# Later residual stores, and another split of the up and gate products in a two-layer decoder trunk

## The chip, the core and the metric

The kernel runs on one core of one Trainium2 chip. The metric is the device time of one execution in microseconds (us). Before the change three executions took 2463.84 us in the median (2461.32 to 2466.27). A further execution was recorded by the hardware profiler; the times in the views below are of that one. The engines are named as the profile names them: PE (matrix products), PEld (its weight loads), DVE (elementwise work and 32x32 transposes), ACT (activations and copies), POOL (here the issuing of small transfers) and SP (the issuing of large ones).

## The reference

Two layers, each with two residual additions, over 256 positions of width 2048 in float32. The mixer half of a layer projects the normed input with `w_in`, runs windowed attention and a spatial gating unit, merges the two by gates, and adds `merged @ w_out` to x. The half that the change touches is this:

```
h2 = rms_norm(x, ffn_norm[l])
x = x + (jax.nn.silu(h2 @ w_gate[l]) * (h2 @ w_up[l])) @ w_down[l]
```

`w_gate` and `w_up` are 2048 x 5632, `w_down` is 5632 x 2048.

## The kernel before, in words

Precision. Each float32 operand is split into a high part and the rest (`whi`/`wlo` for weights, `uh`/`ul` for activations), and each product is three matmuls: high by high, rest by high, high by rest (lines 399, 400, 401). ACT makes `whi` by a copy (line 256), DVE makes `wlo` by a subtraction (line 264). The weights come from memory once and are split once, so for each 256 x 512 piece of weight there is one ACT operation, one DVE operation and a run of matmuls.

Jobs, units, parts. The work is a list of jobs. A wide job multiplies all 256 positions by 1024 columns of a weight, in units of 512 rows (four units for a weight with 2048 rows). A unit is done in one of two ways. Plain: four quarters, each of 12 matmuls of 128x512. Or by a seven-product scheme in the manner of Strassen: seven products of 6 matmuls each, 42 in place of 48. For that the weight's blocks must be added first: four DVE operations of 128x1024 (line 240), and there are seven splits in place of four. The activations need sums too (`sh`, `sl`, lines 520 to 508), made once for a unit and used by all jobs that take that unit in seven products. A job's `m` says how many of its units are done so; they come first, in an order given by `HEAD` and `TAIL`, with the four sums of a unit placed by `SUM_AT` some parts ahead of their use. A job with m=0 has 192 matmuls, with m=1 186, with m=2 180. I call the products and the quarters parts; a part's `whi` and `wlo` are made ahead of PE, as far as 6 and 5 buffers go.

The half that is touched. The columns of gate and up are taken in rounds of 4, 4 and 3 blocks of 512 (`ROUNDS`), with blocks counted f = 0 to 10. In a round come pairs: gate for blocks f and f+1, then up for the same blocks; the last block (f = 10) has gate and up in one job. After the pairs of a round two down jobs add into x. The gate's results leave PSUM through ACT (line 1088), the up's through DVE (line 1094); the result `hid` is transposed in 32x32 blocks by DVE (line 483, tile `blk`), and 16 small transfers issued by POOL (line 489, tile `tt`) put the blocks in their places. ACT and DVE split what arrived (lines 587 and 590, or 511 to 523 with the sums).

The residual before it. The two jobs of `merged @ w_out` add into the four 512-column pieces of x on DVE (line 997). Each piece is then transposed and gathered in the same manner (`blk`, `tt`), scaled on ACT (line 583) and split into one unit of h2 (`uh`, `ul`); all four units are needed by the first gate job. The first two also get their sums. Each piece is stored in memory by SP (`keep_x`, line 359, tile `kept`) and fetched again for the next residual (line 356).

Order. The order of each engine's instructions is fixed by the program. A clock of slots ticks one for each quarter and a half for each product; `after(n, fn)` puts an operation n slots later in every engine's order. How late the second piece of a job is evicted and transposed depends on the m of the next job (`behind`, with `T1_LATE` and `UNIT_LATE`). SP's queue holds the weight loads (line 220), which wait for one of 5 buffers, and between them the stores and fetches of x, in one order.

Of the kernel before, what the change touches and what calls it, by code (L numbers as in the profile page):

```python
# [31 lines left out]
CW2 = 2 * CW  # L32
# [5 lines left out]
N_BIG = 25  # L38
G_BUSY, G_LAND = 3.5, 3
T1_LATE, THEN_LATE, UNIT_LATE = (1.5, 3), (3, 7), (3, 3)  # L40
Q_FIRST = 15
Q_STEP = 4
LOAD_BY = (1, 2, 3, 4)
ROUNDS = ((0, 1, 2, 3), (4, 5, 6, 7), (8, 9, 10))
M_OUT, M_FFN, M_DOWN = (0, 1), (2, 1, 1), 1
M_Q = 0
M_GATE, M_ATT, M_SGU = (1, 1, 1, 1), (0, 0), (1, 0)
M_V, M_U = 1, 1
# [4 lines left out]
def hybrid_trunk(ctx: ExitStack, tc: tile.TileContext, x, mix_norm, w_in, q_norm, k_norm, sinks,  # L53
# [37 lines left out]
    NF = FF // CW  # L91
# [16 lines left out]
    sums, uses = {}, []  # L108
# [51 lines left out]
    for l in range(DEPTH):  # L160
        wl = w_in[l]
        for o in (0, None)[::-1 if l == 0 else 1]:
            add_job([wl[:, o:o + CW2]], m=M_Q * l) if o is not None else add_job([wl[:, O_KV:O_KV + CW]])
        for o, m in ((O_V, M_V), (O_U, M_U), (O_GATE, M_GATE[0]), (O_GATE + CW2, M_GATE[1])):
            add_job([wl[:, o:o + CW2]], m=m)
        add_job([wl[:, O_GATE + D:O_GATE + D + CW2]], m=M_GATE[2])
        for i, o in enumerate((0, CW2)):
            add_job([w_attn_branch[l, :, o:o + CW2]], m=M_ATT[i])
        add_job([wl[:, O_GATE + D + CW2:O_GATE + 2 * D]], m=M_GATE[3])
        for i, o in enumerate((0, CW2)):  # L170
            add_job([w_sgu_branch[l, :, o:o + CW2]], m=M_SGU[i])
        for i, o in enumerate((0, CW2)):
            add_job([w_out[l, :, o:o + CW2]], m=M_OUT[i])
        for fs in ROUNDS:
            for f in fs[::2]:
                if f + 1 < NF:
                    for w, m in zip((w_gate, w_up), M_FFN if f else (1, 1)):
                        add_job([w[l, :, f * CW:(f + 2) * CW]], m=m)
                else:
                    add_job([w[l, :, f * CW:(f + 1) * CW] for w in (w_gate, w_up)], m=M_FFN[2])  # L180
            for o in (0, CW2):
                add_job([w_down[l, :, o:o + CW2]], units=list(fs), m=M_DOWN)

    needed = {}
    for i, n in uses:
# [109 lines left out]
    def after(n, fn):  # L295
        steps.append((slot_no[0] + n, fn))
# [53 lines left out]
    def rows(v):  # L350

        return v.rearrange("(t p) n -> p t n", p=P)
# [5 lines left out]
    def keep_x(c):  # L358
        nc.sync.dma_start(rows(kept[c]), xt[c])
        home[c] = kept[c]  # L360
# [403 lines left out]
    class Attention:  # L764
# [62 lines left out]
        def begin(self):  # L827
            n = Q_FIRST
            for c in range(2):
# [139 lines left out]
    def residual(units, nxt, sums, out_at=None, scale=None):  # L969

        for j in range(0, NCH, 2):

            def done(c, ps, j=j):
                o = j + c

                square_at = 5 if c == 0 else behind(2, 2, 5)

                def then():
                    nxt.unit(o, sums=o < sums)
                    after(square_at, lambda: nxt.squares(o))  # L980
                    if o == NCH - 1:
                        after(square_at + 1, lambda: nxt.finish())

                evicting(c, lambda t: added(o, t, ps), then if nxt is not None else None, late_then=UNIT_LATE)
                if out_at is None:
                    after(7 if c == 0 else 8, lambda: keep_x(o))

            def added(o, t, ps):
                n = 2 if out_at is not None and o == NCH - 1 else 1
                w = CW // n  # L990
                for i in range(n):
                    sl = slice(i * w, (i + 1) * w)
                    d, src = xt[o][:, t, sl], ps[t][:, sl]
                    if scale is None:
                        nc.vector.tensor_tensor(out=d, in0=src, in1=d, op=ALU.add)  # L995
                    else:
                        nc.vector.scalar_tensor_tensor(out=d, in0=src, scalar=scale, in1=d, op0=ALU.mult, op1=ALU.add)  # L997
                    if out_at is not None:
                        eng = nc.sync if i == 0 else nc.scalar
                        eng.dma_start(out_at[0, t * P:(t + 1) * P, o * CW + i * w:o * CW + (i + 1) * w], d)  # L1000

            job = jobs[job_no[0]]
            length = 3.5 * job.m + 4 * (len(job.units) - job.m)
            after(length - 8, lambda j=j: fetch_x(j))
            after(length - 6, lambda j=j: fetch_x(j + 1))
            run(units, done)

    prepare(0)

    for l in range(DEPTH):  # L1010
# [69 lines left out]
        nxt = Norm(mix_cols(l + 1)) if l + 1 < DEPTH else None  # L1080
        for i, fs in enumerate(ROUNDS):
            hid, hT = {}, {}
# [7 lines left out]
            def up_done(f, c, ps):  # L1090
                a = hid[f]

                def upped(t):
                    nc.vector.scalar_tensor_tensor(out=a[:, t, :], in0=ps[t], scalar=norm.r[t], in1=a[:, t, :],
                                                   op0=ALU.mult, op1=ALU.mult)

                evicting(c, upped, lambda: transposed(hT, f, a, on_pe=f == NF - 1, sums=f in fs[:M_DOWN]))

            for f in fs[::2]:
                if f + 1 < NF:  # L1100
# [48 lines left out]
```

## Time and profile before

| what | value |
|---|---|
| median of three executions | 2463.84 us (2461.32 to 2466.27) |
| the profiled execution | 2466.55 us, span 2464.6 us, granted PE clock 0.997 |
| PE busy | 2443.4 us, 10950 matmuls |
| DVE busy | 1990.1 us (81%) |
| ACT busy | 1429.3 us (58%) |
| POOL busy | 475.0 us (19%) |
| read from and written to memory | 492.04 MB, 16.78 MB |

A busy PE is not PE at its peak: matmuls overlap, and a record of 0.39 us can follow the one before it after 0.23 us. So the distance between starts says more than busy time. A window's row gives for each engine the busy time and the count of instructions in it, then the granted PE clock (1.00 is full), the share of the transfer engines that were at work, and GB/s. In a row of the timeline the bracket at the end is the idle time of the engine before it and who ended it.

### The profile page before, as it was taken

To read this page: it belongs to the slowest core of one execution; us is meant where nothing else is said; L and a number is where in the kernel's file an instruction comes from. 1 tells how busy PE (TensorE), PEld (TensorE's weight loads), DVE (VectorE), ACT (ScalarE), POOL (GpSimd) and SP (SyncE) were. 2 spreads that over 40 slices of the span, in tenths; PEclk is the share of its full clock that TensorE was granted. 3 is DMA by queue.
4 is the path that set the end of the run, shared out by engine and by line. 5 is a ranking of instruction groups with operands and counts; after the bars stand their busy time and mean duration, and the time that the engine had idled before them with its cause. 6 is when DMAs were issued, how large, how long until landed. Compare 5 with 4: busy or idle time off the path is not lost. (4 is left out here: it accounts for less than half of the span.)

```text
span 2464.6 us, 30889 instructions
## 1 busy us (share of the span) xinstructions
PE 2443.4 (99%) x10950; PEld 2012.3 (82%) x10950; DVE 1990.1 (81%) x2189; ACT 1429.3 (58%) x1758; POOL 475.0 (19%) x903
## 2 busy tenths in 40 slices
PE   9999999999999999999999999999999999999999
PEld 7888888877888888888888888887778888888887
DVE  7898768786978797788879976777869787978786
ACT  6575545475655665465666665554756555655653
POOL 1421300441220022002235022014402200220020
PEclk9999999999999999999999999999999999999999
DMA  8555556776576757666776546566856757575764
GB/s 311 195 202 190 165 188 218 225 251 216 213 242 205 256 197 243 226 248 198 267 262 218 184 165 201 190 202 205 284 197 222 239 194 263 209 238 190 260 205 166
DMA packets 179051, 539.20 MB, mean 219 GB/s; under 512 B 23872, under 2 KB 26544, under 8 KB 178896
## 3 DMA queue, kind: packets, MB, share of 16 engines
q1 hardware_dynamic: 150832, 508.51, 60.5%
q0 software_dynamic: 27744, 28.44, 3.8%
q8 instruction: 86, 1.41, 0.2%
q14 instruction: 69, 0.57, 0.1%
q10 hardware_dynamic: 320, 0.27, 0.0%
HBM read 492.04 MB, written 16.78 MB: 206 GB/s over the span
## 5 line engine op out<-in xcount | busy, mean ns | idle before, releaser
L264 DVE TENSOR_TENSOR wlo<-raw,whi 128x1024 fp32r<-128x1024 f32 (+1 forms) x956 | 1150.5, 1219 | 381.6 <-PE acc L400 278.6
L256 ACT ACTIVATE whi<-raw 128x1024 fp32r<-128x1024 f32 (+1 forms) x956 | 997.2, 1057 | 692.8 <-PE acc L401 611.9
L399 PE MATMUL acc<-whi,uh 128*128 128x512 f32 x3004 | 1178.0, 392 | 6.8 <-ACT uh L587 4.2
L400 PE MATMUL acc<-wlo,uh 128*128 128x512 f32 x3004 | 1171.1, 390 | 2.4 <-DVE wlo L264 2.4
L401 PE MATMUL acc<-whi,ul 128*128 128x512 f32 x3004 | 1171.7, 390 | 1.4 <-DVE ul L590 1.2
L489 POOL DMA_DIRECT2D tt<-blk x800 | 392.1, 497 | 1682.6 <-DVE blk L483 665.4
L399 PEld LDWEIGHTS acc<-whi,uh 128*128 128x128 f32 x3004 | 565.1, 188 | 128.9 <-ACT uh L587 5.5
L401 PEld LDWEIGHTS acc<-whi,ul 128*128 128x128 f32 x3004 | 565.0, 188 | 121.4 <-DVE ul L590 3.3
L400 PEld LDWEIGHTS acc<-wlo,uh 128*128 128x128 f32 x3004 | 565.2, 188 | 119.8 <-DVE wlo L264 4.0
L399 PE MATMUL acc<-whi,sh 128*128 128x512 f32 x464 | 182.4, 393 | 2.8 <-ACT acc L435 2.2
L256 ACT ACTIVATE whi<-sum 128x1024 fp32r<-128x1024 f32 x116 | 122.8, 1058 | 102.1 <-PE acc L401 87.0
L400 PE MATMUL acc<-wlo,sh 128*128 128x512 f32 x464 | 181.6, 391 | 0.0
L401 PE MATMUL acc<-whi,sl 128*128 128x512 f32 x464 | 181.4, 391 | 0.0
L264 DVE TENSOR_TENSOR wlo<-sum,whi 128x1024 fp32r<-128x1024 f32 x116 | 141.3, 1218 | 6.1 <-PE acc L400 6.1
L399 PEld LDWEIGHTS acc<-whi,sh 128*128 128x128 f32 x464 | 87.5, 188 | 25.7 <-ACT acc L435 6.6
L435 ACT ACTIVATE acc<-acc 128x512 f32<-128x512 f32 x150 | 88.4, 589 | 28.7 <-PE acc L401 20.2
L401 PEld LDWEIGHTS acc<-whi,sl 128*128 128x128 f32 x464 | 87.5, 189 | 18.4
L400 PEld LDWEIGHTS acc<-wlo,sh 128*128 128x128 f32 x464 | 87.5, 189 | 18.0 <-DVE wlo L264 0.3
L590 DVE TENSOR_TENSOR ul<-tt,uh 128x1024 fp32r<-128x1024 f32 x36 | 44.0, 1223 | 42.8 <-ACT uh L587 37.6
L240 DVE TENSOR_TENSOR raw<-raw,sum 128x1024 f32<-128x1024 f32 x58 | 71.0, 1225 | 2.0
L240 DVE TENSOR_TENSOR sum<-raw,raw 128x1024 f32<-128x1024 f32 x58 | 71.0, 1224 | 1.4
L240 DVE TENSOR_TENSOR sum<-raw 128x1024 f32<-128x1024 f32 x58 | 70.7, 1219 | 0.0
(126 smaller groups left out, 1044.5 us busy)
## 6 DMA issues: line engine op xcount, KB each, us to landing
raw<-in_w_in_dram SPq DMA_DIRECT2D x112, 1024.0 KB, 5.5
raw<-in_w_down_dram SPq DMA_DIRECT2D x88, 1024.0 KB, 6.3
raw<-in_w_gate_dram SPq DMA_DIRECT2D x80, 1024.0 KB, 6.3
raw<-in_w_up_dram SPq DMA_DIRECT2D x80, 1024.0 KB, 6.4
raw<-in_w_out_dram SPq DMA_DIRECT2D x32, 1024.0 KB, 6.9
tt<-blk POOLq DMA_DIRECT2D x800, 32.0 KB, 4.9
raw<-in_w_attn_branch_dram SPq DMA_DIRECT2D x16, 1024.0 KB, 6.0
raw<-in_w_sgu_branch_dram SPq DMA_DIRECT2D x16, 1024.0 KB, 5.7
```

Of the source, the lines that this page charges most:

```text
L240: nc.vector.tensor_tensor(out=self.raw(dst), in0=self.raw(one), in1=self.raw(two), op=ALU.subtract)
L256: nc.scalar.activation(hi[:, k, :], raw[:, k, :], AF.Copy)
L264: nc.vector.tensor_tensor(out=lo[:, k, :], in0=raw[:, k, :], in1=hi[:, k, :].bitcast(F32), op=ALU.subtract)
L399: nc.tensor.matmul(ps, a, hi, start=first, stop=False, skip_group_check=True)
L400: nc.tensor.matmul(ps, a, lo, start=False, stop=False, skip_group_check=True)
L401: nc.tensor.matmul(ps, b, hi, start=False, stop=last, skip_group_check=True)
L435: nc.scalar.activation({"11": x, "t2": e, "t3": y}[name], a, AF.Copy)
L489: nc.gpsimd.dma_start(blocks(d)[:, :, i] if whole else d[:, i].rearrange("p k t c -> p (k t) c"), src)
L590: nc.vector.tensor_tensor(out=blocks(unit.lo), in0=tv, in1=blocks(unit.hi).bitcast(F32), op=ALU.subtract)
```

## The change

Three things in the table and two in the code. `keep_x` is put 20 slots after a piece of x is done in place of 7 or 8, in the residuals that feed a norm (the one in the middle of each layer, and the one at the end of the first layer); the others keep 7 and 8. The first gate job of each layer (f = 0) has m=0 in place of 1. The up jobs of f = 0, 2 and 6 have m=2 in place of 1; those of f = 4 and 8 keep 1, and all later gate jobs keep 2. The down jobs' m is now given one by one, with the same values as before.

```diff
+KEEP_LATE = 20
-M_OUT, M_FFN, M_DOWN = (0, 1), (2, 1, 1), 1
+M_OUT, M_FFN, M_DOWN = (0, 1), (2, 2, 1), ((1, 1), (1, 1), (1, 1))
+UP_TWO = (0, 2, 6)
-        for fs in ROUNDS:
+        for fs, ms in zip(ROUNDS, M_DOWN):
             for f in fs[::2]:
                 if f + 1 < NF:
-                    for w, m in zip((w_gate, w_up), M_FFN if f else (1, 1)):
+                    for w, m in ((w_gate, M_FFN[0] if f else 0), (w_up, M_FFN[1] if f in UP_TWO else 1)):
                         add_job([w[l, :, f * CW:(f + 2) * CW]], m=m)
...
-            for o in (0, CW2):
-                add_job([w_down[l, :, o:o + CW2]], units=list(fs), m=M_DOWN)
+            for o, m in zip((0, CW2), ms):
+                add_job([w_down[l, :, o:o + CW2]], units=list(fs), m=m)
...
                 if out_at is None:
-                    after(7 if c == 0 else 8, lambda: keep_x(o))
+                    after(KEEP_LATE if nxt is not None else 7 if c == 0 else 8, lambda: keep_x(o))
...
-                evicting(c, upped, lambda: transposed(hT, f, a, on_pe=f == NF - 1, sums=f in fs[:M_DOWN]))
+                evicting(c, upped, lambda: transposed(hT, f, a, on_pe=f == NF - 1, sums=f in fs[:max(M_DOWN[i])]))
```

The changed file has two more lines near its top, so its line numbers are higher by two: line 264 is 266, 240 is 242, 997 is 999 and so on.

The order moves on DVE where the first gate job begins. `x_4471` (after the change `x_4470`) is the third piece of x, `blk` its transpose, `wlo` the rests of weight parts, `sum` and `raw` as results are the sums of weight blocks, `sums` and `sl` belong to the activations' sums. Before:

```order
L240 TENSOR_TENSOR raw_4380<-raw_4412,sum_4521 128x2x512
L520 TENSOR_TENSOR sums_4375<-tt_4355 128x256
L520 TENSOR_TENSOR sums_4375<-sums_4375,tt_4355 128x256
L520 TENSOR_TENSOR sums_4375<-tt_4355 128x256
L520 TENSOR_TENSOR sums_4375<-tt_4355,sums_4375 128x256
L264 TENSOR_TENSOR wlo_4582<-sum_4521,whi_4559 128x1024
L240 TENSOR_TENSOR sum_4521<-raw_4412,raw_4380 128x1024
L264 TENSOR_TENSOR wlo_4600<-raw_4380,whi_4580 128x1024
L997 SCALAR_TENSOR_TENSOR x_4471<-acc_4273,x_4471 128x512
L997 SCALAR_TENSOR_TENSOR x_4471<-acc_4275,x_4471 128x512
L508 TENSOR_TENSOR sl_4354<-sums_4375,sh_4353 128x1024
L483 STREAM_TRANSPOSE blk_4620<-x_4471 128x4x4x32 x2
```

Now:

```order
L522 TENSOR_TENSOR sums_4375<-tt_4355 128x256
L522 TENSOR_TENSOR sums_4375<-sums_4375,tt_4355 128x256
L522 TENSOR_TENSOR sums_4375<-tt_4355 128x256
L522 TENSOR_TENSOR sums_4375<-tt_4355,sums_4375 128x256
L266 TENSOR_TENSOR wlo_4576<-raw_4380,whi_4554 128x1024
L266 TENSOR_TENSOR wlo_4595<-raw_4412,whi_4574 128x1024
L999 SCALAR_TENSOR_TENSOR x_4470<-acc_4273,x_4470 128x512
L999 SCALAR_TENSOR_TENSOR x_4470<-acc_4275,x_4470 128x512
L510 TENSOR_TENSOR sl_4354<-sums_4375,sh_4353 128x1024
L485 STREAM_TRANSPOSE blk_4615<-x_4470 128x4x4x32 x2
```

The four weight sums of the first gate job are gone from ahead of the third piece: two of them in these rows, the others three and six rows ahead of the first row shown. Behind it, the transposes of the fourth piece follow after five rows now, and after eleven before.

The second place is DVE at the border between the gate and the up job of f = 2. `wlo_5614` is the first part of the up job before, `ul` the split of an earlier `hid`. Before:

```order
L240 TENSOR_TENSOR sum_5583<-raw_5446 128x1024
L264 TENSOR_TENSOR wlo_5595<-raw_5410,whi_5579 128x1024
L240 TENSOR_TENSOR raw_5446<-raw_5459,raw_5446 128x2x512
L264 TENSOR_TENSOR wlo_5614<-raw_5446,whi_5593 128x1024
L240 TENSOR_TENSOR raw_5446<-raw_5459,sum_5583 128x2x512
L264 TENSOR_TENSOR wlo_5631<-sum_5583,whi_5612 128x1024
L240 TENSOR_TENSOR sum_5583<-raw_5459,raw_5446 128x1024
L264 TENSOR_TENSOR wlo_5651<-raw_5446,whi_5629 128x1024
L264 TENSOR_TENSOR wlo_5668<-raw_5459,whi_5649 128x1024
L590 TENSOR_TENSOR ul_5508<-tt_5509,uh_5507 128x1024
L264 TENSOR_TENSOR wlo_5692<-raw_5446,whi_5666 128x1024
```

Now, from just behind the up job's first part (`wlo_5608`) to its seventh (`wlo_5710`):

```order
L242 TENSOR_TENSOR raw_5438<-raw_5451,sum_5558 128x2x512
L266 TENSOR_TENSOR wlo_5625<-raw_5525,whi_5606 128x1024
L242 TENSOR_TENSOR raw_5525<-raw_5578,sum_5590 128x2x512
L266 TENSOR_TENSOR wlo_5645<-sum_5558,whi_5623 128x1024
L266 TENSOR_TENSOR wlo_5662<-sum_5590,whi_5643 128x1024
L242 TENSOR_TENSOR raw_5525<-raw_5578,raw_5525 128x2x512
L592 TENSOR_TENSOR ul_5500<-tt_5501,uh_5499 128x1024
L266 TENSOR_TENSOR wlo_5687<-raw_5438,whi_5660 128x1024
L242 TENSOR_TENSOR sum_5558<-raw_5451,raw_5438 128x1024
L266 TENSOR_TENSOR wlo_5698<-raw_5525,whi_5685 128x1024
L242 TENSOR_TENSOR sum_5590<-raw_5578,raw_5525 128x1024
L266 TENSOR_TENSOR wlo_5710<-raw_5451,whi_5696 128x1024
```

Eight sums of weights now stand where four stood. Behind the gate job's last part but two the order is now: sum, `sl`, part, sum, part, sum, first up part, and then the rows shown.

The third place is SP's queue before the first gate job's end. Before:

```order
L220 DMA raw_4412<-in_w_gate_dram 128x2x1024
L359 DMA kept_100<-x_4101 128x2x512
L220 DMA raw_4456<-in_w_gate_dram 128x2x1024
L356 DMA x_4471<-in_x_dram 128x2x512
L359 DMA kept_101<-x_4136 128x2x512
L356 DMA x_4511<-in_x_dram 128x2x512
```

Now:

```order
L222 DMA raw_4680<-in_w_gate_dram 128x2x1024
L361 DMA kept_100<-x_4101 128x2x512
L222 DMA raw_4737<-in_w_up_dram 128x2x1024
L361 DMA kept_101<-x_4136 128x2x512
L222 DMA raw_4790<-in_w_up_dram 128x2x1024
```

The first two stores stood behind the second and the third load of the first gate job; now they stand behind its eighth and last, and behind the first load of the up job after it. The other two have moved from behind the second and third load of that up job to behind its sixth and eighth.

## The prediction

> **What bounds the kernel now.** I read the page first, for the engine that is always busy.
>
> ```profile
> span 2464.6 us, 30889 instructions
> PE 2443.4 (99%) x10950; PEld 2012.3 (82%) x10950; DVE 1990.1 (81%) x2189; ACT 1429.3 (58%) x1758; POOL 475.0 (19%) x903
> ```
>
> PE is never idle for long, so the end moves only with the number of matmuls, their pace, and PE's waits. To see these job by job I found where each job begins by counting the matmuls of lines 399 to 401 in order of time (186 for a job with m=1), and asked for the windows of the two layers' first jobs behind the residual. Columns: window, length, PE, PEld, DVE, ACT and POOL busy, granted clock, share of the transfer engines, GB/s.
>
> ```profile
> 535.07:586.20 51.13, 46.75 (x188) 36.83 (x187) 38.92 (x44) 32.00 (x45) 17.54 (x34) 0.93 0.62 206
> 586.20:628.43 42.23, 42.23 (x188) 34.84 (x186) 32.93 (x31) 22.68 (x25) 1.10 (x3) 1.00 0.58 199
> 628.43:669.23 40.80, 40.80 (x182) 33.80 (x180) 40.70 (x42) 28.40 (x31) 14.62 (x30) 1.00 0.65 233
> 669.23:711.46 42.23, 42.23 (x187) 34.84 (x186) 31.58 (x30) 22.68 (x25) 1.10 (x3) 1.00 0.60 199
> 711.46:753.62 42.16, 42.16 (x187) 34.91 (x186) 34.46 (x33) 23.53 (x25) 14.57 (x30) 1.00 0.77 249
> ...
> 1759.05:1810.47 51.42, 46.83 (x187) 36.46 (x186) 39.29 (x45) 31.85 (x45) 17.44 (x34) 0.93 0.61 205
> 1893.47:1936.16 42.69, 42.69 (x187) 34.77 (x186) 32.27 (x30) 23.36 (x26) 1.10 (x3) 1.00 0.59 197
> ```
>
> The rows are gate and up of f = 0, gate and up of f = 2 and a down job in the first layer, then gate of f = 0 and up of f = 2 in the second. A down job with 186 matmuls takes 42.16, a gate job with 180 takes 40.80: 0.2267 us a matmul, 1.36 a product, 2.72 a quarter, and PE waits for nothing there. Only the gate job of f = 0 does: 51.13 and 51.42, so 8.97 and 9.26 above 42.16. PE's timeline says where.
>
> ```profile
> 540.68 0.50 PE L400 MATMUL acc<-wlo,uh 128*128 128x512 f32 x1 [0.73 <-DVE wlo L264]
> ...
> 541.72 0.39 PE L401 MATMUL acc<-whi,ul 128*128 128x512 f32 x1
> 543.09 0.67 PE L399 MATMUL acc<-whi,sh 128*128 128x512 f32 x1 [0.98 <-ACT acc L435]
> 543.56 0.63 PE L400 MATMUL acc<-wlo,sh 128*128 128x512 f32 x1
> 543.99 0.63 PE L401 MATMUL acc<-whi,sl 128*128 128x512 f32 x1
> ...
> 570.42 0.39 PE L401 MATMUL acc<-whi,ul 128*128 128x512 f32 x1
> 572.82 0.50 PE L399 MATMUL acc<-whi,uh 128*128 128x512 f32 x1 [2.01 <-ACT uh L587]
> 574.08 0.79 PE L401 MATMUL acc<-whi,ul 128*128 128x512 f32 x1 [0.53 <-DVE ul L590]
> ```
>
> Two waits. **The first**, at the seven products of the first unit, is for DVE, which is behind. **The second** is for the fourth unit of h2, whose gather lands late. Behind both, the pace is half for a while (543.56 to 543.99 is 0.43 us). By starts against 0.2267, the first costs 4.2 and the second 4.6 in this layer; in the other 3.0, 0.5 for the third unit, and 5.8.
>
> **The change, part by part.**
>
> *Matmuls.* Each unit more in seven products saves 6. Per layer the gate of f = 0 loses one such unit (+1.36), three up jobs gain one (3 x -1.36): -2.72, so -5.44 for both.
>
> *First gate job, first wait.* Plain quarters need no weight sums, and each `wlo` has 2.72 us of PE ahead of it, not 1.36. What DVE does now, and POOL, ACT:
>
> ```profile
> 525.09 1.23 DVE L264 TENSOR_TENSOR wlo<-raw,whi 128x1024 fp32r<-128x1024 f32 x1 [2.80 <-ACT whi L256]
> 526.23 1.22 DVE L240 TENSOR_TENSOR raw<-raw,raw 128x1024 f32<-128x1024 f32 x1
> 527.36 1.22 DVE L508 TENSOR_TENSOR ul<-tt,uh 128x1024 fp32r<-128x1024 f32 x1
> ...
> 538.23 1.30 DVE L483 STREAM_TRANSPOSE blk<-x 128x512 f32<-128x512 f32 x2
> 549.75 1.29 DVE L483 STREAM_TRANSPOSE blk<-x 128x512 f32<-128x512 f32 x2
> ...
> 540.16 5.86 POOL L489 DMA_DIRECT2D tt<-blk  x12 [23.44 <-ACT whi L256]
> 547.50 2.03 POOL L489 DMA_DIRECT2D tt<-blk  x4 [1.48 <-DMA tt<-blk]
> 551.59 1.96 POOL L489 DMA_DIRECT2D tt<-blk  x4 [2.06 <-ACT whi L256]
> 561.85 0.98 POOL L489 DMA_DIRECT2D tt<-blk  x2 [0.49 <-DMA tt<-blk]
> ...
> 555.25 1.71 ACT L583 ACTIVATE tt<-tt,vcols 128x256 f32<-128x256 f32 x4 [1.15 <-DMA tt<-blk]
> 569.97 1.71 ACT L583 ACTIVATE tt<-tt,vcols 128x256 f32<-128x256 f32 x4 [6.22 <-DMA tt<-blk]
> 571.71 1.06 ACT L587 ACTIVATE uh<-tt 128x1024 fp32r<-128x1024 f32 x1
> ```
>
> DVE steps of this kind follow each other 1.14 apart (525.09, 526.23). Its rows carry no idle time from there to behind 538.23, and three of the four removed sums lie in that stretch: the third piece's transposes come 3.4 earlier, at 534.8. The new first danger is a PSUM bank: the second quarter's second half, at 535.07 + 4.08 = 539.15, takes the one that the fourth piece's first half leaves. That DVE step stands two `wlo` behind the transposes: 534.8 + 1.3 + 2.3 + 0.7 = 539.1. So it just fits; if not, a few tenths.
>
> *Second wait.* The transposes of the fourth piece now stand five rows behind those of the third, not eleven: 536.1 + 4.7 = 540.8, not 549.75. POOL issues the third piece's 16 transfers from 536.7 (540.16 - 3.4), for 9.4 us as before (to 547.50 + 2.03), then the fourth's from 546.1 for 11.3 us (551.59 to 561.85 + 0.98), and they are there 7.1 later, as before: 564.5. ACT needs 2.8 (569.97 to 572.77): 567.3. With 12 quarters ahead, PE wants the unit at 535.07 + 32.64 = 567.7. The third: 555.25 - 3.4 + 2.8 = 554.6 against a need at 556.8. In the other layer the same steps leave about 1 us and 2 us. So both waits go, narrowly. The stores help or hurt here:
>
> ```profile
> 554.87 0.46 SPq L359 DMA_DIRECT2D kept<-x  x1
> 560.89 0.46 SPq L359 DMA_DIRECT2D kept<-x  x1
> ...
> kept<-x SPq DMA_DIRECT2D x2, 512.0 KB, 9.5
> tt<-blk POOLq DMA_DIRECT2D x23, 32.0 KB, 6.0
> ```
>
> Two stores of 512 KB now land (9.5 us each) inside the fourth piece's gather, whose transfers take 6.0 there. The changed queue issues two others behind the job's last load, near 541 and 545, so they meet the third piece's gather and the start of the fourth's instead; the pair that hurt moves into the up job, where nothing is gathered. That should leave the third piece 1 to 2 us less than computed and the fourth about that much more. I take 0.5 us of leftover waits a layer; bounds: 0, and the second wait whole (4.6 and 5.8).
>
> So the gate job: 51.13 to 192 x 0.2267 = 43.52 + 0.5, and 51.42 to 44.02; -7.1 and -7.4.
>
> *Up jobs.* Each goes to 40.80: the f = 0 and 6 ones from 42.2, the f = 2 ones from 42.23 and 42.69. That is -4.3 and -4.75 a layer, if DVE keeps up. A second unit costs DVE three more parts and four sums, 7 x 1.14 = 8.0: 31.58 becomes 39.6 of 40.80, behind a gate job with 40.70 of 40.80. For f = 0 the job ahead has little of this, so I cost it at nothing. For f = 2 and 6 I counted rows.
>
> ```profile
> 653.42 2.35 DVE L264 TENSOR_TENSOR wlo<-raw,whi 128x1024 fp32r<-128x1024 f32 x2
> 655.69 1.22 DVE L508 TENSOR_TENSOR sl<-sums,sh 128x1024 fp32r<-128x1024 f32 x1
> ...
> 669.56 1.22 DVE L264 TENSOR_TENSOR wlo<-raw,whi 128x1024 fp32r<-128x1024 f32 x1
> ```
>
> From 655.69 the changed order has 18 rows and then the `wlo` of the up job's seventh product: 655.69 + 18 x 1.14 + 1.22 = 677.4. PE, begun at 669.23, wants it at 669.23 + 6 x 1.36 + 0.23 = 677.6; before, the fifth product's was there at 670.8 (669.56 + 1.22), 4.1 ahead of its need at 669.23 + 4 x 1.36 + 0.23. Behind the seventh come parts alone, and DVE gains 0.2 on each. So the margin is nought: I take 0.3 a place, four places, 1.2. Bounds: 0, and the nearest row where DVE was late, the first wait above with its half pace, 3.0 to 4.2.
>
> *End of the first layer.* The stores there move past weight loads into the next layer's first two jobs. Nobody waits for them: the next use of their buffers lies in the third job, some 40 us on, against 9.5 for a landing. 0; without that cover at most one landing.
>
> *Sum.* First layer -7.1 - 4.3, second -7.4 - 4.75, and +1.2: -22.3. The profiled execution would go from 2466.55 (span 2464.6, 1.95 around it) to 2444.2. It is 2.7 above the median 2463.84; from the median the forecast is **2441.5**.
>
> **A rule weighed.** How much a short wait costs depends on the half pace:
>
> ```profile
> 1767.37 0.51 PE L399 MATMUL acc<-whi,sh 128*128 128x512 f32 x1 [0.98 <-ACT acc L435]
> ...
> 544.00:546.00 2.00, 2.00 (x6) 1.63 (x5) 2.00 (x3) 1.50 (x3) 2.00 (x5) 0.50 1.00 395
> 575.00:577.00 2.00, 2.00 (x6) 1.52 (x6) 2.00 (x3) 0.61 (x1) 0.00 (x0) 0.50 0.46 51
> 1766.00:1768.00 2.00, 1.02 (x5) 0.53 (x4) 2.00 (x4) 1.26 (x2) 2.00 (x5) 1.00 0.64 97
> ```
>
> Behind the first layer's two waits the granted clock was 0.50; behind the same 0.98 in the second layer it stayed 1.00. The Trainium skill ("TensorE: Matmul & The Clock Gate", "Part 1: The HAM clock gate") says that the clock follows activity in a free-running window of about 3.4 us; these rows fit. By it every leftover wait here might cost up to 1.7 us (half of an estimated 3.4, from that page) more, and six such would take the sum to about -12; by the rows the forecast's waits, each shorter than the 0.98 that went unpunished in the second layer, cost only themselves.
>
> **Rivals.**
>
> *A. The forecast*, 0.66: 2441.5, its own range 2438 to 2446.
>
> *B. The fourth unit stays late*, 0.14. The margin was 0.4 by the old rates; loads run there too. With the second wait whole, 4.6 + 5.8 less 1.0 taken: 2450.9. Against it: the transposes come 9 us earlier.
>
> *C. DVE is late in the up jobs of f = 2 and 6*, 0.12. For it: 40.70 of 40.80 and a margin of 0.2. Four waits like the first one, 3.0 to 4.2 less 0.3: +11 to +16, taken as 13.5: 2455.
>
> *D. The change does not do what it says*, 0.04: both waits return in the first gate job and only the matmuls count, 2463.84 - 5.4 = 2458.4, or less with C: no change that can be told.
>
> *E. Slower*, 0.04: in the first ten products of those up jobs DVE is late again and again, and the clock stays halved for all 60 matmuls, 60 x 0.2 = 12 a place, 48 in all: 2441.5 - 1.2 + 48 = 2488. It decides from 6 us a place, 30 matmuls at half pace; a slower PE lets DVE catch up, which speaks against it.
>
> **How the numbers follow.** A, B and C are faster by over 0.2% (4.9 us, about what a measurement of this kernel can tell from no change): 0.92. D is the same, 0.04; E slower, 0.04. The range holds A, B and half of C: 2437 to 2455.
>
> **What would show it.** The window of the first gate job: 43.5 to 44.5 us at clock 1.00, with no wait for `uh` at its thirteenth part; 50 would be B, or D. The third piece's transposes some 3 us and the fourth's some 9 us earlier against the job's start. The up jobs of f = 0, 2 and 6: 40.8 each, with DVE busy for nearly all of it; 43 or more for f = 2 and 6 is C. A wait for PSUM (an `acc` released by line 999) over 1 us in the second quarter, or a gather over 2 us slower under the moved stores, would prove me wrong on the path of the first gate job.

## The result, and the profile after

The changed kernel takes 2443.18 us in the median of four executions (2442.93 to 2445.95), the kernel before 2463.39 on the same chip (2461.32 to 2466.27). The ratio is 0.992, with a 95% interval of 0.9903 to 0.9937: faster, by 20.2 us or 0.8%. The forecast was 2441.5, with a range of 2437 to 2455. The profiled execution took 2442.93 us (span 2441.2), the one before 2466.55 (span 2464.6), which is 3.2 above its kernel's median; so what is read from these two profiles, 23.6 us, is more than the medians give. Its page begins:

```profile
span 2441.2 us, 30915 instructions
...
PE 2428.7 (99%) x10926; PEld 2004.8 (82%) x10926; DVE 2015.1 (83%) x2213; ACT 1441.9 (59%) x1762; POOL 474.2 (19%) x903
```

PE has 24 matmuls less (10950 before), DVE has 24 rows more (2189 before). The windows of the changed kernel, with the columns explained ahead of the prediction: gate and up of f = 0, gate and up of f = 2 in the first layer, then the first job of the second layer, its gate of f = 0 and its up of f = 2.

```profile
535.36:578.90 43.54, 43.54 (x193) 36.00 (x192) 30.52 (x35) 27.22 (x38) 16.87 (x34) 1.00 0.65 218
578.90:619.70 40.80, 40.80 (x181) 33.78 (x180) 38.02 (x36) 25.46 (x27) 0.00 (x0) 1.00 0.63 232
619.70:661.15 41.45, 41.16 (x182) 33.63 (x180) 41.35 (x43) 28.89 (x31) 15.75 (x32) 1.00 0.64 229
661.15:703.32 42.17, 41.39 (x182) 33.63 (x181) 39.83 (x38) 26.13 (x28) 1.10 (x3) 1.00 0.54 200
...
1225.36:1268.88 43.52, 43.52 (x194) 36.04 (x193) 31.31 (x39) 28.36 (x40) 16.84 (x35) 1.00 0.76 255
...
1746.83:1790.35 43.52, 43.52 (x194) 36.05 (x192) 31.19 (x36) 27.32 (x38) 16.84 (x34) 1.00 0.65 223
1871.95:1913.61 41.66, 41.15 (x182) 33.70 (x180) 39.32 (x37) 27.38 (x30) 1.10 (x3) 1.00 0.55 202
```

Both first gate jobs stand at 192 times 0.2267 us, at full clock: nothing is left of 8.97 and 9.26 us. What was not forecast is in the third and fourth row (a gate job of 41.45, an up job of 42.17) and in the fifth (43.52, where the kernel before took 44.63). Job by job, by the distances between first matmuls, with the run "once more" of the same kernel (told below) beside it:

| job | before | forecast | after | once more |
|---|---|---|---|---|
| layer 1: gate f = 0 | 51.13 | 44.0 | 43.55 | 43.52 |
| up f = 0 | 42.23 | 40.8 | 40.80 | 40.80 |
| gate f = 2 | 40.80 | 40.8 | 41.45 | 40.80 |
| up f = 2 | 42.23 | 41.1 | 42.17 | 40.99 |
| up f = 6 | 42.23 | 41.1 | 40.97 | 40.98 |
| layer 2: first job | 44.63 | 44.6 | 43.52 | 43.52 |
| out, first half | 45.70 | 45.7 | 44.57 | 44.55 |
| out, second half | 42.69 | 42.7 | 42.16 | 42.48 |
| gate f = 0 | 51.43 | 44.0 | 43.52 | 45.34 |
| up f = 0 | 42.20 | 40.8 | 40.80 | 40.80 |
| up f = 2 | 42.69 | 41.1 | 41.66 | 41.19 |
| up f = 6 | 42.23 | 41.1 | 40.97 | 40.96 |
| sum against before | | -22.4 | -24.1 | -24.3 |

The rest of the spans' difference (23.4 and 22.9 shorter) is nearly all in the first job of the program, 0.5 and 1.2 longer in these two executions, in the last, 0.4 longer in both, and in the first out job of the first layer, 0.3 shorter in both.

The changed kernel's timeline, DVE's transposes of the third and fourth piece and ACT's rows behind the two gathers:

```profile
534.42 1.30 DVE L485 STREAM_TRANSPOSE blk<-x 128x512 f32<-128x512 f32 x2
...
540.21 1.29 DVE L485 STREAM_TRANSPOSE blk<-x 128x512 f32<-128x512 f32 x2
...
553.11 1.71 ACT L585 ACTIVATE tt<-tt,vcols 128x256 f32<-128x256 f32 x4 [2.84 <-DMA tt<-blk]
...
564.18 1.71 ACT L585 ACTIVATE tt<-tt,vcols 128x256 f32<-128x256 f32 x4 [5.43 <-DMA tt<-blk]
565.93 1.06 ACT L589 ACTIVATE uh<-tt 128x1024 fp32r<-128x1024 f32 x1
```

The prediction had 534.8, 540.8, 551.8 and 564.5 for the first four of these rows. The fourth unit is there at 567.0, and PE needs it at 535.36 + 32.64 = 568.0.

### The profile page after: what moved, and what is told of

Its sections match the earlier page's. It is cut to its first block, busy times and chain, and to the rows that moved or that the text cites. A ratio compares the mean times of both kernels' runs of the same rounds, so it can differ in the third digit from the quotient of the medians.

```text
span 2441.2 us, 30915 instructions
## 1 busy us (share of the span) xinstructions
PE 2428.7 (99%) x10926; PEld 2004.8 (82%) x10926; DVE 2015.1 (83%) x2213; ACT 1441.9 (59%) x1762; POOL 474.2 (19%) x903
## 5 line engine op out<-in xcount | busy, mean ns | idle before, releaser
L401 PE MATMUL acc<-whi,uh 128*128 128x512 f32 x2964 | 1160.2, 391 | 1.6 <-DVE gate L1061 1.5
L402 PE MATMUL acc<-wlo,uh 128*128 128x512 f32 x2964 | 1154.2, 389 | 2.6 <-DVE wlo L266 2.6
L403 PE MATMUL acc<-whi,ul 128*128 128x512 f32 x2964 | 1153.9, 389 | 0.2 <-DVE ul L550 0.2
L401 PEld LDWEIGHTS acc<-whi,uh 128*128 128x128 f32 x2964 | 556.4, 188 | 120.3 <-issue 2.3
L402 PEld LDWEIGHTS acc<-wlo,uh 128*128 128x128 f32 x2964 | 556.6, 188 | 118.7 <-DVE wlo L266 5.2
L401 PE MATMUL acc<-whi,sh 128*128 128x512 f32 x496 | 193.4, 390 | 0.0
L402 PE MATMUL acc<-wlo,sh 128*128 128x512 f32 x496 | 193.2, 390 | 0.2 <-DVE wlo L266 0.2
L403 PE MATMUL acc<-whi,sl 128*128 128x512 f32 x496 | 193.1, 389 | 0.0
L266 DVE TENSOR_TENSOR wlo<-sum,whi 128x1024 fp32r<-128x1024 f32 x124 | 150.4, 1217 | 4.2 <-PE acc L402 4.2
L403 PEld LDWEIGHTS acc<-whi,sl 128*128 128x128 f32 x496 | 93.1, 188 | 19.5
L242 DVE TENSOR_TENSOR raw<-raw,raw 128x1024 f32<-128x1024 f32 x62 | 75.6, 1219 | 1.7 <-DMA raw<-in_w_gate_dram 1.7
```

The lines of the kernel that those rows point to most:

```text
L242: nc.vector.tensor_tensor(out=self.raw(dst), in0=self.raw(one), in1=self.raw(two), op=ALU.subtract)
L266: nc.vector.tensor_tensor(out=lo[:, k, :], in0=raw[:, k, :], in1=hi[:, k, :].bitcast(F32), op=ALU.subtract)
L401: nc.tensor.matmul(ps, a, hi, start=first, stop=False, skip_group_check=True)
L402: nc.tensor.matmul(ps, a, lo, start=False, stop=False, skip_group_check=True)
L403: nc.tensor.matmul(ps, b, hi, start=False, stop=last, skip_group_check=True)
```

## The experiments

Twelve runs, each beside the kernel before on the same chip; the trace of a run is one execution of it. The theory going in (T) was that of the prediction: the table of products removes both waits in the first gate job, the stores only ease transfers. The first rival (S) was that the stores do it.

**The stores alone.** Before's table, and

```diff
-                    after(7 if c == 0 else 8, lambda: keep_x(o))
+                    after(KEEP_LATE if nxt is not None else 7 if c == 0 else 8, lambda: keep_x(o))
```

> The kernel before with the later stores alone; the table of products as before. Theory T (the table does the work at the first gate job, the stores only ease transfers elsewhere): the gate jobs of f = 0 keep both waits and stay at 50 to 52 us each, the first wait (DVE late) at about 4.2 and 3.0; the first job of the second layer loses its wait of 1.1 us and its first out job one of 1.1, so about 2461 (2459 to 2463). Rival S (the stores, out of the way of the fourth piece's gather, free the fourth unit): the second wait goes, 4.6 and 5.8 us, so about 2451 to 2453.

Measured: 2459.36 us against 2465.40, ratio 0.9978 (0.9969 to 0.9987). The windows of the two gate jobs of f = 0 and, between them, the first job of the second layer:

```profile
534.84:582.49 47.65, 44.12 (x187) 34.36 (x186) 39.48 (x45) 32.04 (x46) 16.99 (x34) 1.00 0.64 221
1231.05:1274.57 43.52, 43.52 (x194) 36.04 (x193) 31.17 (x39) 28.27 (x40) 16.84 (x35) 1.00 0.72 240
1754.98:1803.04 48.06, 44.21 (x187) 34.36 (x186) 38.97 (x44) 31.53 (x45) 17.51 (x34) 1.00 0.64 219
```

Neither theory had this. By starts the second wait shrinks to 1.1 and 1.5 us, the first stays (3.2 and 2.7), and the third unit comes late by 1.0 and 1.5: 47.65 and 48.06, where T said 50 to 52 and S some 46. ACT begins on the fourth unit 33.0 us into the first of these jobs (34.9 before, 569.97 less 535.07): enough for most of the wait, not for all. So the stores alone give 3.5 and 3.4 us in these jobs, and 1.1 in the second layer's first job, as T said.

**The table alone.** The changed kernel with the old line for the stores (7 or 8 slots).

> The changed kernel with the stores where they stood before: the table of products alone. Theory T: the gate jobs of f = 0 at 43.5 to 44.5 us with no wait above 0.5; the extra wait of the first layer's gate job of f = 2 (41.45 with the stores late) is gone, 40.8; the second layer's first job is back at 44.6 and its first out job at 45.7; in sum about 2444 to 2447. Rival S: the fourth unit is late again in both gate jobs by 3 us or more with what follows it, so 2450 or more.

Measured: 2445.94 us against 2465.40, ratio 0.9929 (0.9916 to 0.9941). Right in the sum, but not in its parts: in the profile the first layer's gate job is down to 44.63, the second layer's is not. This profile is the slowest of the five executions (2449.81; three took 2444.8 to 2445.9), so the waits that follow are larger than those of most. The windows of the second layer's first job and of that gate job, and then PE's waits in the latter (us in total, times, longest):

```profile
1224.06:1270.30 46.24, 44.40 (x193) 35.80 (x192) 32.55 (x40) 29.65 (x41) 16.84 (x35) 1.00 0.69 231
1748.24:1797.67 49.43, 46.03 (x193) 36.95 (x192) 34.20 (x39) 27.19 (x38) 16.82 (x34) 0.97 0.65 208
```

```profile
PE acc L401 <- ACT uh L589: 1.8, 1, 1.8
PE acc L401 <- DVE x L999: 1.1, 1, 1.1
PE acc L403 <- DVE ul L592: 0.5, 1, 0.5
```

The fourth unit is late again, and a wait for PSUM (released by the residual add) stands ahead of it. The timeline of this kernel shows a store beside the fourth piece's gather:

```profile
1759.53 0.46 SPq L361 DMA_DIRECT2D kept<-x  x1
...
1773.09 1.31 SPq L361 DMA_DIRECT2D kept<-x  x1
...
1781.38 1.71 ACT L585 ACTIVATE tt<-tt,vcols 128x256 f32<-128x256 f32 x4 [8.29 <-DMA tt<-blk]
```

The second of these stores is issued while the fourth piece is gathered. ACT begins on that piece 33.1 us into the job; in the run "once more", with the stores elsewhere, at 29.8 (1775.78 less 1746.00), and it must begin by 29.8 (32.64 less its own 2.8). So in this execution the second layer's gate job gets 2.0 of its 7.9 us without the stores' move, the first layer's 6.5 of 7.6. By the medians the table alone gives 19.5 us and the stores alone 6.0, against 20.2 for both (21.3 in the run "once more"): the two overlap, and beside the table the stores are worth 1 to 2 us, which the intervals do not tell from nothing. In the first layer's gate job of f = 2 no wait is left, as T had it.

**The first pair only.**

```diff
-UP_TWO = (0, 2, 6)
+UP_TWO = (0,)
```

> The changed kernel with two units in seven products only in the up job of f = 0, one in those of f = 2 and 6. Theory T: these four jobs go back to 42.2 each (they took 42.17, 40.97, 41.66 and 40.97, together 165.8; now 168.7 to 169.4), all else stays: 2443.2 + 3 to 3.6, about 2446 to 2447. The wait of the first layer's gate job of f = 2 for a load stays (41.4) if it comes from the moved stores. Rival R (two units there cost DVE as much as they save PE, in those jobs and the ones behind them): 2443 to 2444.

Measured: 2449.28 us against 2465.40, ratio 0.9939 (0.9926 to 0.9953). That is 16.1 below the kernel before; the changed kernel was 20.2 below, so the second unit at f = 2 and 6 is worth some 4 us: T, and R falls. The load wait of the gate job of f = 2 was there for DVE (0.9 us), but did not reach PE in that job (40.80); behind it the up job took 42.64.

**The up jobs of f = 2 and 6 only.**

```diff
-                    for w, m in ((w_gate, M_FFN[0] if f else 0), (w_up, M_FFN[1] if f in UP_TWO else 1)):
+                    for w, m in ((w_gate, M_FFN[0] if f else 1), (w_up, M_FFN[1] if f in UP_TWO else 1)):
-UP_TWO = (0, 2, 6)
+UP_TWO = (2, 6)
```

> Stores late and two units in the up jobs of f = 2 and 6; the first pair as before the change (one unit each in gate and up of f = 0). Theory T (DVE's wait in the up job of f = 2 is the price of that job and the gate job ahead of it): the excess of the up jobs of f = 2 over 40.80 stays at 0.7 to 1.4 us and of f = 6 near 0.2; both waits of the first gate job are there, 50 to 52 each; total 2461 less 3.6, about 2457 (2455 to 2459). Rival I (DVE comes late into f = 2 because the up job of f = 0 had two units): the excess at f = 2 falls to that of f = 6, 0.2, and the total to about 2455.

Measured: 2453.69 us against 2465.40, ratio 0.9955 (0.9943 to 0.9968), lower than T had it. Gate of f = 0, up of f = 2, and the second layer's gate of f = 0:

```profile
535.05:583.01 47.96, 45.14 (x188) 35.65 (x186) 39.35 (x45) 32.17 (x45) 16.88 (x34) 0.96 0.63 220
666.01:706.99 40.98, 40.98 (x182) 33.71 (x180) 38.64 (x37) 25.89 (x28) 1.10 (x3) 1.00 0.57 206
...
1751.36:1801.72 50.36, 45.49 (x188) 35.58 (x186) 40.32 (x45) 32.97 (x46) 16.77 (x34) 0.97 0.60 209
```

Late stores without the plain first gate job leave the first wait whole (4.6 and 4.1 by starts) and some of the second (1.0 and 3.7): 47.96 and 50.36. The up job of f = 2 is 40.98 in the first layer, an excess of 0.18 over 180 matmuls, as at f = 6: here I has the number, but not the cause, since with the table alone that job took 41.00 behind an up job of f = 0 with two units. In the second layer it keeps 0.67, but there the waits are for ACT, and with one unit the job had 0.53 before. So 1.37 was not DVE's price of the second unit; the next runs show what it was.

**The changed kernel once more, and the second unit elsewhere.** Four kernels on one chip: `UP_TWO` as (0, 4, 8), as (0, 2, 4, 6, 8), as (0, 4, 6, 8), and unchanged.

> The changed kernel itself once more, as the control on this chip. Theory L (the moved stores make DVE wait for the loads of the gate job of f = 2 in the first layer, and that wait reaches PE only when it is long): DVE again waits there for 0.9 to 1.9 us, the job takes 40.8 to 41.5 and the up job behind it 41 to 42.2; the time is 2443 within 2. Rival V (the wait of the first profile was an accident of that execution alone): no wait for a load there at all.

Once more: 2442.91 us (2442.20 to 2443.45) against 2464.16. Its windows of up f = 2 in the first layer and gate f = 0 in the second, and PE's wait in the latter:

```profile
661.16:702.16 41.00, 41.00 (x182) 33.71 (x180) 38.65 (x37) 25.91 (x28) 1.10 (x3) 1.00 0.56 206
...
1746.00:1791.34 45.34, 43.84 (x193) 35.96 (x192) 33.86 (x38) 27.35 (x39) 16.81 (x34) 1.00 0.67 230
```

```profile
PE acc L401 <- DVE x L999: 1.5, 1, 1.5
```

In this execution DVE has no wait for a load in the first layer's jobs of f = 0 and 2, and the up job of f = 2 takes 40.99. In the first profile it had, and PE paid twice; DVE's waits there and PE's rows where a `wlo` came late:

```profile
DVE raw L242 <- DMA raw<-in_w_gate_dram: 1.5, 1, 1.5
...
DVE sum L242 <- DMA raw<-in_w_gate_dram: 0.3, 1, 0.3
```

```profile
628.54 0.50 PE L402 MATMUL acc<-wlo,uh 128*128 128x512 f32 x1 [0.29 <-DVE wlo L266]
...
670.77 0.50 PE L402 MATMUL acc<-wlo,uh 128*128 128x512 f32 x1 [0.62 <-DVE wlo L266]
```

So L's claim that the wait comes each time is wrong, and V's that it was a single accident is wrong too. Over all the runs: where DVE waited for a load of that gate job in the first layer (1.8, 0.9, 1.0, 0.7 and 1.6 us in five executions, all with the plain first gate job and stores 20 slots late), the excess of the up job of f = 2 was 1.37, 0.48, 0.54, 0.80 and 1.40; in the nine others it was 0.06 or 0.07 with one unit there (three) and 0.16 to 0.20 with two (six). In the second layer DVE waited for these loads in seven of the eight executions with that first gate job and that place of the stores (0.2 to 1.4 us). With other places for the stores or another first pair the wait never came, in either layer (six executions).

The loads show what the stores do. Behind the last two stores the first two loads of the gate job of f = 2 took 10.5 and 13.1 us from issue to landing in the first profile and 10.5 and 13.0 once more, but 7.1 and 8.4 with the table alone. In the first profile they were also issued 2 us later in the layer (58.1 us behind the start of the first gate job, once more 56.2). Only the two together made the wait of 1.8; what makes those 2 us, no run tells.

> The changed kernel with the second unit in seven products in the up jobs of f = 0, 4 and 8 (f = 2 and 6 back at one). Theory D (an up job has its own allowance of DVE: behind the gate jobs of f = 4 and 8, with DVE busy 35.0 of 40.8 us, a second unit is free): the up jobs of f = 4 and 8 take 40.8 each, with no wait, those of f = 2 and 6 42.2 to 43; in sum 1 to 2 us below the changed kernel run beside it, about 2442. Rival N (DVE's total is the limit: what it is late then comes out in the next gate job or the next down job): waits of 0.5 to 1.4 us behind f = 4 and 8, and the time of the changed kernel or up to 3 us more.

Measured: 2442.90 us, ratio to before 0.9913 (0.9898 to 0.9928), the same as once more. D is right about up of f = 4 and 8: they take 40.80 in both layers, without a wait, and nothing comes later behind them. The gain of 1 to 2 us in the sum went to another place: the second layer's up job of f = 2, with one unit, took 44.35 here, with a wait of 1.6 us for ACT's step on a PSUM tile (line 437).

> The changed kernel with two units in seven products in the up jobs of all even f. Theory D: the up jobs of f = 4 and 8 from 42.2 to 40.8 in both layers, the rest as in the changed kernel: 5.7 us below it, about 2437.5. Rival N (the allowance is a total; up f = 4 at about 41 of 40.8 us of DVE now stands ahead of gate f = 6 with 40.7): DVE late in gate and up of f = 6 by 1 to 3 us a layer, so 0 to 3 us below.

Measured: 2438.74 us (2437.96 to 2438.88), ratio to before 0.9895 (0.988 to 0.991), 4.2 below the changed kernel beside it. The up jobs of f = 4 and 8, first layer, and the second layer's gate of f = 0:

```profile
825.75:866.55 40.80, 40.80 (x181) 33.80 (x180) 38.01 (x36) 25.80 (x28) 1.35 (x3) 1.00 0.56 208
1073.42:1114.22 40.80, 40.80 (x181) 33.78 (x180) 36.33 (x34) 25.79 (x28) 0.98 (x2) 1.00 0.58 207
...
1743.58:1788.86 45.28, 43.85 (x193) 35.96 (x192) 34.26 (x39) 27.33 (x38) 16.78 (x34) 1.00 0.66 229
```

The four jobs give their 5.7 us; the second layer's first out job, 1.66 longer in this execution, takes some of it back. N falls: gate and up of f = 6 are at 40.80 and 40.95. This kernel is below both kernels of the case.

> As the run with all even f, with the up job of f = 2 back at one unit. If the second unit at f = 2 is worth its 1.36 us in spite of the waits there (it stood at 42.17 and 41.66 against 42.2 to 43.4 with one unit), this is 1 to 2 us slower than the run with all even f, about 2439; if DVE's wait there eats the gain, the same time, about 2437.5.

Measured: 2441.37 us, ratio 0.9905 (0.989 to 0.992), 2.6 above the one with all even f. The second unit at f = 2 pays in spite of the waits there. With one unit that job took 42.70 and 44.31, with two 40.96 and 41.80.

**Where the stores cost.** Two more places, both with all even f in `UP_TWO`, and that kernel again as their control. `KEEP_LATE = 30` puts two stores behind the fifth load of the up job of f = 0 and two behind the fifth load of the gate job of f = 2. `KEEP_LATE = 14` puts two among the last loads of the first gate job and two into the up job's.

> The kernel with two units in the up jobs of all even f, its stores of the middle residual later still: all behind the loads of the first up job and in the loads of gate f = 2, so that none is issued during the gathers of the first gate job. Theory G (a store costs by landing within a gather): the gate jobs of f = 0 as without this (43.5 and 43.5 to 45.3, whose wait for PSUM comes from the gather ahead of the job, where no store stands either), the fourth piece's gather lands at most 1 us earlier; total within 1.5 us of its control. Rival Q (a store costs by holding up the loads behind it on its queue): the loads of the up and gate jobs behind come late, DVE waits for them by over 2 us in the first layer and the job of gate or up f = 2 takes 1 to 2 us more a layer; 2 to 4 us slower.

> The kernel with two units in the up jobs of all even f, two of its stores of the middle residual earlier, between the last loads of the first gate job (ahead of and at the start of its gathers), the other two at its end. Theory G: the stores land while the third piece is gathered or before, the fourth is hit little; gate jobs of f = 0 at 43.5 to 45.5, total within 2 us of the control. Rival Q: the two stores delay the last loads of gate f = 0 and DVE with them: waits for loads in the gate job, or for PSUM (released by the residual add) of 1 to 3 us in either layer; 2 to 5 us slower.

> The kernel with two units in the up jobs of all even f once more, as the control on this chip: 2438.7 within 1.5 us; the excess of the gate job of f = 0 in the second layer anywhere from 0 to 1.8 us, of the up jobs of f = 2, 4, 6 and 8 at most 0.2 (0.4 to 1.0 for f = 2 of the second layer).

Measured: 2435.33 us (2434.41 to 2437.54) with 30, 2438.03 (2436.47 to 2438.97) with 14, 2438.40 (2435.53 to 2438.96) for the control; ratios to before 0.9877, 0.9887 and 0.9886, whose intervals overlap. So the times do not tell the three apart. The control's up job of f = 2 had an excess of 0.80 in the first layer, beyond the 0.2 expected, behind a load wait. The timelines tell more. With 30, first layer, SP's next stores and ACT's start on the fourth unit:

```profile
567.01 0.98 SPq L361 DMA_DIRECT2D kept<-x  x2
```

```profile
558.08 1.70 ACT L585 ACTIVATE tt<-tt,vcols 128x256 f32<-128x256 f32 x4
```

With no store in its gather the fourth piece is there 22.9 us into the job (558.08 less 535.15); in the control it is 28.5, in the changed kernel 28.8 (564.18 less 535.36), and 26.7 to 28.8 in all eight executions with the plain gate job and 20 slots. I had expected at most 1 us of this. So by this one execution the stores still cost that gather 4 to 6 us in the first layer, and PE does not see it because ACT need begin on the piece only 29.8 us into the job. With 14 it is 26.7, though the last of the stores ahead of it had landed 20 us earlier. In the second layer it is 28.6, within the 27.3 to 30.3 of the eight: there the gather is as late without a store, and no run tells by what. Q falls in its size: with 30 and with 14 there is no load wait in the gate job of f = 2 at all. That wait belongs to the place that `KEEP_LATE = 20` gives the last two stores.

**The end of the first layer.** The term that I had costed at nothing, undone by itself:

```diff
-                    after(KEEP_LATE if nxt is not None else 7 if c == 0 else 8, lambda: keep_x(o))
+                    after(KEEP_LATE if scale is not None else 7 if c == 0 else 8, lambda: keep_x(o))
```

> The changed kernel with the four stores at the end of the first layer where they stood before; those of the middle residual stay late. Theory G (a store costs by lengthening the gather it lands in, and the gather's lateness reaches the first job of the second layer through DVE and PSUM, or through the fourth unit): that job goes from 43.5 to between 44.6 and 46.3 us, as in the two kernels with those stores early, and the total is 1 to 3 us above the changed kernel, 2444 to 2446; nothing else moves by more than these places do from one execution to the next. Rival O (the prediction's: nobody waits for these stores, their move is worth nothing; the 1.1 us came from elsewhere): the job stays at 43.5 to 44.1 and the total at 2443.

Measured: 2446.04 us (2444.60 to 2446.55) against 2465.85, ratio 0.9921 (0.9907 to 0.9934); once more was at 2442.91, on another chip with a ratio of 0.9912, so the times do not tell the two apart. The job does. The first job of the second layer in this kernel, and PE's waits in it:

```profile
1225.06:1271.56 46.50, 44.39 (x193) 35.80 (x192) 32.44 (x40) 29.52 (x41) 16.78 (x35) 1.00 0.68 228
```

```profile
PE acc L401 <- DVE x L997: 0.8, 1, 0.8
PE acc L401 <- ACT uh L589: 0.8, 1, 0.8
PE acc L403 <- DVE ul L592: 0.5, 1, 0.5
```

46.50 against 43.52: 3.0 us, 0.2 above what G allowed. Over all executions this job took 43.5 to 44.2 us with those stores late (eleven) and 44.6, 46.2 and 46.5 with them early (three): O falls. The timeline of this kernel shows two stores and ACT's start on the fourth piece, and the second fence the same rows of the run once more:

```profile
1238.82 0.46 SPq L361 DMA_DIRECT2D kept<-x  x1
...
1247.44 0.47 SPq L361 DMA_DIRECT2D kept<-x  x1
...
1256.89 1.71 ACT L585 ACTIVATE tt<-tt,vcols 128x256 f32<-128x256 f32 x4 [7.69 <-DMA tt<-blk]
```

```profile
1240.43 0.48 SPq L361 DMA_DIRECT2D kept<-x  x1
...
1245.53 0.47 SPq L361 DMA_DIRECT2D kept<-x  x1
...
1248.92 1.71 ACT L585 ACTIVATE tt<-tt,vcols 128x256 f32<-128x256 f32 x4 [1.64 <-DMA tt<-blk]
```

The late stores are in this job too: the early ones are issued 13.8 and 22.4 us into it, the late ones 16.2 and 21.3. The fourth piece is there at 31.8 with the early stores and at 24.7 with the late (24.7 to 28.7 in the nine executions with 20 slots at this place); in the run with 30, whose first store comes 42.5 us into the job, it is there at 23.8. With the early stores it was there at 28.3, 31.6 and 31.8 in the three executions. Which share of the 7 us comes from the 2 us of place inside the job, and which from the two early stores ahead of it (at 1206.78 and 1214.29), no run tells. The Trainium skill ("DMA: Bandwidth & Descriptors", "Issuing engines are not separate DMA queues") says that transfers run on the same 16 engines and interleave, whichever engine issued them; that POOL's gathers end later beside SP's stores here agrees with it.

## Why the prediction was right, and where it was not

*Matmuls, -5.44.* As computed: 24 less.

*The first gate job, -7.1 and -7.4.* Right: -7.6 and -7.9 in the profile, -7.6 and -6.1 once more. The working holds: against the job's start the third piece's transposes are 4.1 us earlier than before (3.4 forecast) and the fourth's 9.8 (9.0), the fourth unit ready 1.0 ahead of its need (0.4). The 0.5 us of leftover waits was put in the wrong place. The fourth unit was on time in every kernel with both the table and the late stores, but for 0.5 us in one. What came in its stead is what the prediction named as the first new danger and costed at a few tenths: the PSUM bank behind the residual add, in the second layer 0 to 1.8 us from one execution to the next, 1.5 in the run once more. Over 1 us was the prediction's own sign of being wrong on this path, and in that execution it is met.

*The stores' share of it.* Right in direction, wrong in size. I said that they "help or hurt" by 1 to 2 us. Alone they gave 3.5 and 3.4; the table alone 6.5 and, in its slowest execution, 2.0. The two overlap in the first layer; in the second they needed each other in that execution, and by the medians not in most. That the transposes' 9 us would free the fourth unit (the argument against rival B) held in the first layer of the table alone only narrowly: ACT began on it 30.0 us into the job, with 29.8 needed, and the job lost 1.1. In the second, rival B is what that execution shows.

*The up jobs, -9.05 + 1.2.* Right at f = 0 and 6: 40.80, and 0.17 at each f = 6 (0.3 forecast). DVE's 8.0 us for the second unit were 7.1 (31.58 to 38.65). At f = 2 the term failed: 1.37 and 0.86 in place of 0.3 each, and 0.65 in the first layer's gate job ahead. The step that failed is the count of 18 rows from 655.69 on: it took DVE's start in the gate job as it was before. The stores that I had moved "into the up job, where nothing is gathered" meet the loads of the gate job of f = 2 there, DVE waited up to 1.8 us for them, and with a margin of nought all of it came out at PE. Once more DVE stood at the place where the count begins 13.5 us ahead of the up job, as before the change (669.23 less 655.69), and the job took 40.99; in the first profile it stood there 12.3 ahead. Without that wait the term is 0.2 in the first layer, and the forecast of 0.3 good.

*The end of the first layer, 0.* Wrong, by 1.1 us against the kernel before, and by 3.0 in the changed kernel. The step said that nobody waits for these stores. The gathers that feed the next layer's first job run beside them and end later for it, and PE waits for those. I had used this mechanism one paragraph earlier for the middle residual and not here.

*The second layer's out jobs.* Not forecast: -1.1 and -0.5. In the executions of this study the first took 44.6 (eight) or 45.0 to 46.7 (six), and no edit goes with it throughout; the runs leave open why.

*Rivals.* C has the late engine, but not the cause or the size: DVE's wait for its own work is 0.2 a place, and at f = 2 it was late for a load, by up to 1.4 us and not 3.0 to 4.2. E falls: no clock was halved in an up job. B and D did not happen in the changed kernel. So the forecast was near by more than its own steps: forecast -22.4, measured by jobs -24.1, of which 0.65 + 1.07 + 0.56 were lost at f = 2, and 1.1 + 1.7 gained at places costed at nothing. That these nearly cancel is luck. So is some of the sum's nearness: by the medians the gain is 20.2 (21.3 once more), and the profile before, from which its rows were read, was 3.2 us slower than its kernel's median. Which of its waits were longer than usual, one trace does not show.

## What to carry to other kernels

A large transfer that nobody waits for is not free: ask which small transfers run beside it, and how much slack the one who waits for those has; here the place of two or four stores of 512 KB moved the end of a gather by up to 6 us in the first layer's gate job (22.9 to 28.8) and by up to 8 at the end of the layer (23.8 to 31.8). When two edits act on the same wait, cost each with and without the other: alone the stores gave 6.0 us, beside the table some 1 to 2, if any. A profile is one execution: look where it lies among the times of its kernel before reading a wait as typical. A count of an engine's rows gives its margin only if the place where the count begins stays put; a load that comes 1 us later moves it, and where the margin is nought all of it reaches the end (with two units at f = 2; with one, 0.4 to 0.5 of some 1.0 us did).

## What was not expected of the hardware

How a wait is punished by the clock. After one wait of up to 1.8 us (the wait of 1.6 in an up job, by starts) the granted clock stayed at 1.00 in every case. After two waits close together that made 1.9 us or more by starts, it was halved in six of ten cases, for 7 to 12 matmuls, and the same pair was punished in one execution and not in the next; in one of the six it was halved within the first of the two already, which was 2.35 us long. From the run with the up jobs of f = 2 and 6 only: behind 0.8 and 1.0 in the second layer's gate job, and behind 1.1 and 0.5 later in the same job:

```profile
1760.00:1762.00 2.00, 1.20 (x5) 1.03 (x6) 2.00 (x3) 1.84 (x3) 2.00 (x5) 1.00 0.67 134
1790.00:1792.50 2.50, 2.50 (x7) 1.93 (x6) 2.50 (x3) 1.10 (x2) 0.00 (x0) 0.50 0.33 39
```

And from the run once more, behind its one wait of 1.5:

```profile
1751.00:1753.00 2.00, 1.25 (x5) 1.05 (x6) 2.00 (x4) 0.00 (x0) 2.00 (x5) 1.00 0.96 216
```

The clock records of the traces show what decides it. Apart from the one at the program's end, where PE has no more work, each halving lasts 3.41 us or twice that, and within a trace all changes of the clock lie whole multiples of 3.413 us apart: in the kernel before, the three halvings begin at 543.26, 573.98 and 1795.95, which are 9 and 367 such steps. I cut each of the fourteen traces into stretches on this grid and added up PE's idle time in each (from a matmul's end, at most 0.227 us behind its start, to the next start). The six stretches just ahead of these halvings have 2.03 to 2.88 us of it; no other stretch at full clock, from the first clock record on, has more than 1.95. So here the clock was halved when PE stood idle for about six tenths of such a stretch or more. A pair of waits that falls on both sides of a boundary goes free: that of the second layer in the kernel before, whose 0.98 the prediction shows, is cut at 1765.23 into 0.97 and 1.33.

The price of a short wait therefore depends on where it falls on a grid that a program does not choose. Before a run it is a chance: 0.2 us a matmul for some ten matmuls, or nothing.
